# A two-layer trunk on one core: MLPs in groups of three pairs with products and up blocks in turn, and the attention's weights split in the first MLP

## The chip, the cores and the metric

The kernel runs on one core of a Trainium2 chip. The metric is the time of one execution on the device in microseconds, the median of the runs; lower is better. The kernel is written in Tile: a planner puts each engine's instructions in an order at build time and adds the semaphores, and on the chip every engine takes its instructions in that order.

Engines, as the profile names them: PE is TensorE (matmuls; PEld its weight loads), DVE is VectorE, ACT is ScalarE, POOL is GpSimd, SP is SyncE, which here issues all DMAs.

## The reference

The input is 512 tokens of 1024 channels, all float32. Layer 0 mixes tokens by pooling, layer 1 by stick-breaking attention with 16 heads of 64; each mixer is followed by an MLP with a hidden width of 4096. Every part has an RMS norm before and after it.

```python
def sq_relu_mlp(h, w_up, w_down):
    u = jnp.matmul(h, w_up)
    return jnp.matmul(jnp.square(jax.nn.relu(u)), w_down)
...
    for layer in range(DEPTH):
        h = rms_norm(x, mix_pre_g[layer])
        if layer < N_A:
            m = pool_mixer(h, pool_w[layer], pool_scale[layer])
        else:
            q = jnp.matmul(h, w_q[j]).reshape(B, S, N_HEADS, HEAD_DIM).transpose(0, 2, 1, 3)
            o = stick_breaking_attention(q, k, v)
            m = jnp.matmul(o.transpose(0, 2, 1, 3).reshape(B, S, HD), w_o[j])
        x = x + rms_norm(m, mix_post_g[layer])
        h = rms_norm(x, mlp_pre_g[layer])
        x = x + rms_norm(sq_relu_mlp(h, w_up[layer], w_down[layer]), mlp_post_g[layer])
        if layer == N_A - 1:
            kv = jnp.matmul(rms_norm(x, kv_norm_g), w_kv).reshape(B, S, 2, N_HEADS, HEAD_DIM)
...
```

## The kernel before

**Precision.** A float32 operand is split in two fp32r parts, high and low: ACT casts the high part (`split`, line 188, or `weight`, line 118), DVE subtracts it from the source for the low part (lines 189 and 120). Each product is three matmuls: high x high, high x low, low x high.

**Weights of up blocks and of the attention.** `weight` (line 106) loads 512 KB into one of two `raw` buffers (line 108, on SP), multiplies it by a gain on POOL where there is one (line 130, two instructions; the v, k and q weights of the attention have one, the o weights not), casts (118) and subtracts (120). The results go to one of four slots. `queue` holds all weights in the order of their use, first MLP, attention, second MLP; `fill` makes the next one as long as fewer than four are made and not yet used, `get` hands one out. In the attention, `fill` also keeps a weight's instructions behind the latest ones of the main work (`behind`, `gate`).

**An MLP** has 32 up blocks of 128 hidden units. An up block is 24 matmuls of 512 columns (lines 534 to 536), then Relu and Square on ACT (489, 490). The first 28 blocks' down product is done by a Strassen scheme (Winograd's form, seven products in place of eight) in the class `Seven`: seven groups of four blocks, that is of two pairs. The left operands are sums of the squares (tokens halved; lines 403 to 406 on POOL), the right ones combinations of quarters of four w_down blocks (line 423 on DVE), both then split by `split`. `feed` makes the left operands of a group as its up blocks come out, `prepare` the right ones. `add_to` (461) runs a group's seven products in a row: each is 12 matmuls (line 456) into two PSUM banks, followed by two instructions that add the banks to `y` (line 473, DVE; the first touch of a part is a copy on ACT, 471). Between two groups' products stand four up blocks. The last four blocks are multiplied plainly in `contract` (lines 209 to 211), which also runs the layer's end norm and update, tile by tile of 128 tokens. The w_down blocks of a group are loaded into the three `xn` buffers, which the norms use too, and a spare one (lines 382 to 384).

**The start of an MLP.** The first four up blocks are computed in two halves of the tokens, because the norm's last two token tiles are transposed late (`need`). Then comes a fifth up block, and then the first group's seven products.

**The attention** follows a list, `ATT_ORDER` (line 49): V (values), K and P (keys, queries), S (scores, sigmoids, the scan of line 752 on DVE), T (transposes, 770), A (mixing with the values, 780), O and E (output projection through `contract`, PE order kept by hand in E). Its 32 weights (8 each of v, k, q and o) are made one after the other by `fill` as slots come free.

Of the kernel before, what the change touches and what calls it, by code (L numbers as in the profile page):

```python
# [15 lines left out]
P = 128  # L16
D = 1024
# [5 lines left out]
GRP = 4  # L23
HEADS = 16
# [37 lines left out]
def trunk(ctx, tc, x, consts, gcol, grow, pw, wup, wdn, wq, wk, wv, wo, out):  # L62
# [5 lines left out]
    psum = pool("psum", 8, space=bass.MemoryType.PSUM)  # L68

# [19 lines left out]

    def xn_tile():  # L90
        return work.tile([P, D], F32, tag="xn", bufs=3, name=name("xn"))
# [49 lines left out]
    def place(k):  # L141

        if k[0] == "dn":
            return [dn_pool[0].tile([P, D], F32R, tag="w", bufs=8, name=name(x)) for x in "hl"]
        if k == ("o", 6):
            both = att_pool[0].tile([P, 2, D], F32R, tag="v", bufs=2, name=name("w"))
            return [both[:, 0], both[:, 1]]
        if k == ("o", 7):
            return [att_pool[0].tile([P, NSEG], F32R, tag="w", bufs=2, name=name(x))[:, :D] for x in "hl"]
        return [wts.tile([P, D], F32R, tag=f"w{x}", bufs=4, name=name(x)) for x in "hl"]  # L150

    def make():
        k, src, scaled = queue.pop(0)
        on = nc.gpsimd if k in ON_POOL else nc.vector
        made[k] = weight(src, place(k), scaled, on)

    def fill(n=1):
        if gate[0]:
            behind.update(latest)
        for _ in range(n):  # L160
            if queue and len(made) < ahead and (queue[0][0][0] != "dn" or dn_pool[0] is not None):
# [7 lines left out]
    for l in range(2):  # L169
        if l == 1:  # L170
            for what, i, part in ATT_ORDER:
# [6 lines left out]
                elif what == "O" and 0 in part or what == "E":  # L178
                    for c in range(2 * i, 2 * i + (2 if what == "O" else 4)):
                        want(("o", c), wo[c])  # L180
        for j in range(NJ):
# [111 lines left out]
    def contract(lhs, w, y, first, update=None, tiles=range(T), soon=False):  # L293
# [4 lines left out]
        for t in tiles:  # L298
# [26 lines left out]
            else:  # L325
                product(0, range(last + 1))
            evacuate(0)
# [5 lines left out]
            elif normed and t == T - 1:  # L333
                if not soon:
                    ups[0].transpose()
# [26 lines left out]
    class Seven:  # L362
# [11 lines left out]

        PRODUCTS = (
# [4 lines left out]
        def __init__(self, l, g, mp):  # L380
            self.mp, self.rows, self.left, self.right = mp, [], {}, {}
            self.raw = [xn_tile(), xn_tile(), xn_tile(), spare_tile()]
            for j, raw in enumerate(self.raw):
                nc.sync.dma_start(raw, wdn[l, g * GRP + j])
            self.rest = self.prepare()

        def feed(self, r):

            q, second = divmod(len(self.rows), 2)
            self.rows.append(r)  # L390
            tile = lambda n, tag: self.mp.tile([P, 2, n], F32R, tag=tag, bufs=2, name=name(tag))
            lo, hi = slice(0, S // 2), slice(S // 2, S)
            if not second:
                a = self.left["r11", q] = tile(S // 2, "r11")
                split(r[:, lo], a[:, 0], a[:, 1])
                return
            a = tile(S, "r2")
            split(r, a[:, 0], a[:, 1])
            self.left["r12", q], self.left["r22", q] = a[:, :, lo], a[:, :, hi]
            r1 = self.rows[-2]  # L400
            sums = self.mp.tile([P, 2, S], F32, tag="s", name=name("s"))
            s2, s3, s1, s4 = sums[:, 0, lo], sums[:, 0, hi], sums[:, 1, lo], sums[:, 1, hi]
            nc.gpsimd.tensor_tensor(out=s3, in0=r1[:, lo], in1=r1[:, hi], op=ALU.subtract)
            nc.gpsimd.tensor_tensor(out=s1, in0=r1[:, hi], in1=r[:, hi], op=ALU.add)  # L404
            nc.gpsimd.tensor_tensor(out=s2, in0=s1, in1=r1[:, lo], op=ALU.subtract)  # L405
            nc.gpsimd.tensor_tensor(out=s4, in0=r[:, lo], in1=s2, op=ALU.subtract)
            for n, (x, y) in enumerate((("s2", "s3"), ("s1", "s4"))):
                a = tile(S, f"s{n}")
                split(sums[:, n], a[:, 0], a[:, 1])
# [481 lines left out]
```

## Time and profile before

| What | Value |
|---|---|
| Median of 3 runs | 994.76 us (992.62 to 996.26) |
| The profiled execution's own time | 996.64 us |
| Its span, first to last instruction | 994.8 us |
| Mean granted TensorE clock | 0.984 |
| Stages, from the windows | pooling mixer to 56 us; first MLP to 372; attention to about 650; second MLP to the end |

A row of the windows table gives, for a stretch in us from the span's start, each engine's busy time and, in brackets, its number of instructions, then the clock granted to TensorE (1.00 is full), the mean busy share of the 16 DMA engines and GB/s moved. A row of a timeline gives start, duration, engine, line, operation, output<-inputs and, in square brackets, how long the engine sat idle before it and what ended that. A row of one line's durations gives min/median/max in ns.

### The profile page before, as it was taken

The numbers are of one execution on the slowest core, as the hardware profiler recorded it, in microseconds if no ns is written. First come the engines' busy times: TensorE is split into PE (matmuls) and PEld (weight loads), VectorE is DVE, ScalarE is ACT, GpSimd is POOL, SyncE is SP. The second block draws the span as 40 slices with busy tenths as digits, with TensorE's granted clock in tenths as the row PEclk, the third lists the DMA queues.
The fourth block names the chain that finished last, engine by engine and source line by source line (L and its number), as shares of the span: only waits on it lengthen the run. The fifth ranks groups of instructions, "written<-read, shape, count | busy, mean of one in ns | idle before, by whom it ended". The sixth has DMA issues, their size and how long they took to land.

```text
span 994.8 us, 12988 instructions
## 1 busy us (share of the span) xinstructions
PE 954.4 (96%) x4823; PEld 810.8 (82%) x4823; DVE 780.6 (78%) x1067; ACT 557.0 (56%) x1005; POOL 252.2 (25%) x238
## 2 busy tenths in 40 slices
PE   7898999999999999999999999989999999999997
PEld 5896888888888888888788988788888888888886
DVE  5987788878877747488688889989778878888636
ACT  5656546456455446566667576658556455464532
POOL 1642202112021147241252300436212021121103
PEclk8998999999999999999999999999999999999999
DMA  7254323323232230112222221144323233231202
GB/s 267 85 162 135 106 86 107 109 103 106 85 111 81 85 127 22 62 45 64 64 73 69 64 72 65 65 148 149 110 102 111 84 125 105 85 127 64 64 22 85
DMA packets 26991, 94.50 MB, mean 95 GB/s; under 512 B 3120, under 2 KB 3504, under 8 KB 26928
## 3 DMA queue, kind: packets, MB, share of 16 engines
q1 hardware_dynamic: 26928, 93.68, 28.2%
q8 instruction: 38, 0.62, 0.2%
q14 instruction: 25, 0.20, 0.1%
HBM read 91.57 MB, written 2.10 MB: 94 GB/s over the span
## 4 chain that ended last, share of the span: by engine, by line
PE 76%; DVE 8%; ACT 4%; POOL 3%; issue 2%; DMA 1%; POOLq 0%; DVEq 0%; ACTq 0%
PE ps L456 26%; PE ps L535 13%; PE ps L536 13%; PE ps L534 13%; PE ps L209 3%; PE ps L210 2%; PE ps L211 2%; DVE e L752 2%; PE ps L780 1%; DVE l L120 1%; PE ps L770 1%; POOL y L234 1%; DMA xn<-in_wdn 1%; ACT h L118 1%; DVE x L240 1%
## 5 line engine op out<-in xcount | busy, mean ns | idle before, releaser
L535 PE MATMUL ps<-xnl,h 128*128 128x512 f32 (+1 forms) x712 | 262.0, 369 | 4.1 <-DVE xnl L189 4.1
L536 PE MATMUL ps<-xnh,l 128*128 128x512 f32 (+1 forms) x712 | 262.1, 369 | 0.5 <-DVE l L120 0.5
L534 PE MATMUL ps<-xnh,h 128*128 128x512 f32 (+1 forms) x712 | 261.0, 369 | 0.0
L120 DVE TENSOR_TENSOR l<-raw,h 128x1024 fp32r<-128x1024 f32 x101 | 128.8, 1276 | 48.5 <-ACT h L118 48.3
L456 PE MATMUL ps<-w,s 128*128 128x512 f32 x672 | 163.4, 394 | 2.1 <-ACT s L188 1.5
L535 PEld LDWEIGHTS ps<-xnl,h 128*128 128x128 f32 x712 | 134.8, 189 | 26.1 <-DVE xnl L189 4.3
L536 PEld LDWEIGHTS ps<-xnh,l 128*128 128x128 f32 x712 | 134.8, 189 | 22.8 <-DVE l L120 0.7
L456 PEld LDWEIGHTS ps<-w,s 128*128 128x128 f32 x672 | 127.2, 190 | 31.1 <-ACT s L188 2.7
L534 PEld LDWEIGHTS ps<-xnh,h 128*128 128x128 f32 x712 | 134.2, 190 | 21.9
L473 DVE TENSOR_TENSOR y<-ps,y 128x512 f32<-128x512 f32 x180 | 120.1, 688 | 40.5 <-PE ps L456 39.3
L118 ACT CAST h<-raw 128x1024 fp32r<-128x1024 f32 x105 | 110.4, 1053 | 63.9 <-PE ps L535 32.4
L456 PE MATMUL ps<-w,r 128*128 128x512 f32 x504 | 124.3, 390 | 2.4 <-DVE r L189 2.4
L188 ACT CAST w<-t 128x512 fp32r<-128x512 f32 x112 | 69.2, 622 | 80.8 <-PE ps L456 61.0
L456 PEld LDWEIGHTS ps<-w,r 128*128 128x128 f32 x504 | 94.7, 188 | 22.4 <-DVE r L189 2.8
L404 POOL TENSOR_TENSOR s<-r,r 128x256 f32<-128x256 f32 x28 | 28.2, 1008 | 323.9 <-ACT r L490 323.9
L130 POOL TENSOR_TENSOR raw<-raw,gc 128x512 f32<-128x512 f32 x48 | 69.9, 1477 | 145.7 <-DMA raw<-in_wv 68.9
L188 ACT CAST w<-xn 128x512 fp32r<-128x512 f32 x56 | 34.9, 624 | 90.1 <-PE ps L456 80.0
L189 DVE TENSOR_TENSOR w<-t,w 128x512 fp32r<-128x512 f32 x112 | 76.5, 705 | 0.7 <-ACT w L188 0.7
L188 ACT CAST s<-s 128x512 fp32r<-128x512 f32 x56 | 34.6, 620 | 45.6 <-POOL s L405 37.6
L189 DVE TENSOR_TENSOR s<-s,s 128x512 fp32r<-128x512 f32 x56 | 42.5, 763 | 22.0 <-ACT s L188 17.5
L189 DVE TENSOR_TENSOR r<-r,r 128x512 fp32r<-128x512 f32 (+1 forms) x60 | 47.2, 789 | 11.7 <-ACT r L188 11.6
L752 DVE TENSOR_TENSOR_SCAN e<-u,begin 128x1280 f32<-128x1280 f32 x16 | 47.5, 2968 | 8.7 <-ACT u L746 8.5
(138 smaller groups left out, 1577.9 us busy)
## 6 DMA issues: line engine op xcount, KB each, us to landing
raw<-in_wup SPq DMA_DIRECT2D x64, 512.0 KB, 3.5
xn<-in_wdn SPq DMA_DIRECT2D x42, 512.0 KB, 3.6
spare<-in_wdn SPq DMA_DIRECT2D x14, 512.0 KB, 4.1
raw<-in_wdn SPq DMA_DIRECT2D x8, 512.0 KB, 3.5
raw<-in_wv SPq DMA_DIRECT2D x8, 512.0 KB, 3.4
raw<-in_wk SPq DMA_DIRECT2D x8, 512.0 KB, 3.5
raw<-in_wq SPq DMA_DIRECT2D x8, 512.0 KB, 3.5
raw<-in_wo SPq DMA_DIRECT2D x8, 512.0 KB, 3.5
```

What stands on the lines that cost most here:

```text
L118: nc.scalar.copy(hi, raw)
L120: on.tensor_tensor(out=lo, in0=raw, in1=hi.bitcast(F32), op=ALU.subtract)
L130: nc.gpsimd.tensor_tensor(out=v[:, h], in0=v[:, h], in1=g[:, h].broadcast_to((P, n // 2, D // n)), op=ALU.mult)
L188: latest["act"] = nc.scalar.copy(hi, src)
L189: latest["dve"] = nc.vector.tensor_tensor(out=lo, in0=src, in1=hi.bitcast(F32), op=ALU.subtract)
L209: nc.tensor.matmul(dst, ah, bh, start=start, stop=False)
L456: nc.tensor.matmul(bank, r[:, a], w_[:, NS[b]], start=start and q == 0 and k == 0, stop=q == 1 and k == 2, skip_group_check=True,)
L473: nc.vector.tensor_tensor(out=part, in0=bank, in1=part, op=ALU.add)
L534: nc.tensor.matmul(pu[:, cols], wh[:, k, :], xnh[:, k, cols], start=k == 0, stop=False)
L535: nc.tensor.matmul(pu[:, cols], wh[:, k, :], xnl[:, k, cols], start=False, stop=False)
L536: nc.tensor.matmul(pu[:, cols], wl[:, k, :], xnh[:, k, cols], start=False, stop=k == KC - 1)
L752: nc.vector.tensor_tensor_scan(out=e[:, ::-1], data0=u[:, 1:][:, ::-1], data1=begin[:, ::-1], initial=0.0, op0=ALU.mult, op1=ALU.max,)
```

## The change

**The MLP.** The 28 blocks of the Strassen part are cut into five groups, of 2, 3, 3, 3 and 3 pairs. The operands of one product for all pairs of a group are now made by single instructions: a left operand is one cast and one subtract over pairs x 256 columns, a right one a combination, a cast and a subtract over pairs x 512. They lie in two buffers each, so that the operands of product i+2 are made while product i+1 waits or runs; before, a group's operands were made in advance of all its products. A product of three pairs is 18 matmuls. After each product comes one up block of the next group, as long as there are any (six for seven products; in the last group the four plain blocks). The left sums are formed in place, four per group as before four per pair. The w_down blocks of a group come by two DMAs, one into an own tile `w1`, one into `xn3`, the three norm buffers in one tile.

**The attention's weights.** In the first MLP, after each product, `split_apart` loads, scales and splits one of the 32 attention weights into a single buffer `apart`; the next call writes it to DRAM (1 MB, both parts) before it takes its own weight. Groups 1 to 3 take a second one after their fourth product. In the attention, `make` only loads the two parts from DRAM (two DMAs of 512 KB) into a slot.

**What goes with it.** A weight's two parts lie in one tile; four plain w_down weights go into operand buffers that the last group has left; the attention keeps its mixed heads in buffers of its own; the DMA scratch is 256 in place of 1024; the first tile's transposes in the last norm are issued a little earlier.

```diff
+GROUPS = (2, 3, 3, 3, 3)
+MOST = max(GROUPS)
...
+    xn3 = work.tile([P, 3, D], F32, tag="xn3", name="xn3")
+    turn = [0]
+
     def xn_tile():
-        return work.tile([P, D], F32, tag="xn", bufs=3, name=name("xn"))
+        turn[0] += 1
+        return xn3[:, turn[0] % 3]
...
+    def split_apart(mp):
+        for both, t in going:
+            nc.sync.dma_start(both, t.bitcast(F32))
+        going.clear()
+        if not apart:
+            return
+        k, src, scaled = apart.pop(0)
+        t = mp.tile([P, 2, D], F32R, tag="apart", name=name("apart"))
+        weight(src, [t[:, 0], t[:, 1]], scaled)
+        kept[k] = dram.tile([P, 2, D], F32, tag=f"kept{len(kept)}", name=name("kept"))
+        going.append((kept[k], t))
 
     def make():
         k, src, scaled = queue.pop(0)
+        if k in kept:
+            made[k] = place(k)
+            for n, t in enumerate(made[k]):
+                nc.sync.dma_start(t.bitcast(F32), kept[k][:, n])
+            return
...
+        def load(self, second):
+            n = self.n
+            if second:
+                w = self.w2 = xn3
+            else:
+                w = self.w1 = self.mp.tile([P, MOST, D], F32, tag="w1", name=name("w1"))
+            src = wdn[self.l, self.first : self.first + 2 * n].rearrange("(n k) p d -> k p n d", k=2)
+            nc.sync.dma_start(w[:, :n], src[1 if second else 0])
...
+        def left(self, i):
+            n, key = self.n, self.PRODUCTS[i][1]
...
+            s1 = self.s1[:, :n]
+            sub = lambda out, x, y, op=ALU.subtract: nc.gpsimd.tensor_tensor(out=out, in0=x, in1=y, op=op)
+            if key == "s3":
+                sub(s1, r21, r22, ALU.add)
+                sub(r21, r11, r21)
+                sub(r11, s1, r11)
+            elif key == "r22":
+                sub(r11, r12, r11)
+            src = {"r11": r11, "s3": r21, "s2": r11, "r22": r22, "s1": s1, "r12": r12, "s4": r11}[key]
+            a = self.mp.tile([P, 2, MOST, S // 2], F32R, tag="a", bufs=2, name=name("a"))
+            split(src, a[:, 0, :n], a[:, 1, :n])
+            return a
+
+        def right(self, i):
...
+            if key == "t3":
+                combine(e, w22, w12)
+            elif key == "t2":
+                combine(e, e, w11, ALU.add)
+            elif key == "t4":
+                combine(e, w21, e)
+            elif key == "t1":
+                combine(w12, w12, w11)
...
+            w = self.mp.tile([P, 2, MOST, 512], F32R, tag="w", bufs=2, name=name("w"))
+            split(src, w[:, 0, :n], w[:, 1, :n])
+            return w
...
     def mlp(l, mp, update):
...
+        groups[0].load(0)
+        groups[0].squares()
         need(0, 1)
...
+        for i in range(2):
+            groups[0].make(i)
+        for g, group in enumerate(groups):
+            coming = groups[g + 1] if g + 1 < len(groups) else None
+            if coming:
+                coming.squares()
+            ups = list(range(firsts[g + 1], firsts[g + 1] + 2 * GROUPS[g + 1]) if coming else range(plain, NJ))
+            for i in range(7):
+                group.product(i, y, written if g == 0 else None)
+                if l == 0:
+                    for _ in range(2 if i == 3 and 0 < g < 4 else 1):
+                        split_apart(mp)
+                if i + 2 < 7:
+                    if ups:
+                        up(ups.pop(0))
+                    group.make(i + 2)
+                    if i + 2 == 4 and coming:
+                        coming.load(0)
+                    if i + 2 == 6 and coming:
+                        coming.load(1)
+                else:
+                    if ups:
+                        up(ups.pop(0))
+                    if coming:
+                        coming.make(i + 2 - 7)
...
```

More of the change, by code (lines that the diff above doesn't have):

```diff
@@ L378, in trunk @@
         )
[L380 to L391, printed above, removed]
-            lo, hi = slice(0, S // 2), slice(S // 2, S)
[L393 to L409, printed above, removed]
-                self.left[x, q], self.left[y, q] = a[:, :, lo], a[:, :, hi]
```

176 lines of the change are left out of this document (83 added, 93 removed).

## The prediction

> **What bounds the kernel now.** I read the page first, for the engines' shares. TensorE (PE) is the bound, 96% busy, VectorE (DVE) follows with 78%; the chain of waits says the same: 76% of it is PE, 8% DVE.
>
> ```profile
> PE 954.4 (96%) x4823; PEld 810.8 (82%) x4823; DVE 780.6 (78%) x1067; ACT 557.0 (56%) x1005; POOL 252.2 (25%) x238
> PE 76%; DVE 8%; ACT 4%; POOL 3%; issue 2%; DMA 1%; POOLq 0%; DVEq 0%; ACTq 0%
> ```
>
> An average hides the stages, so next the table by windows (busy us and count of each engine, granted clock, DMA share, GB/s).
>
> ```profile
> core 0: us, PE busy (x) PEld busy (x) DVE busy (x) ACT busy (x) POOL busy (x), PEclk, DMA share, GB/s
> 56.00:84.00 28.00, 25.04 (x165) 22.24 (x163) 25.34 (x30) 17.45 (x30) 11.90 (x9) 0.97 0.45 145
> 84.00:124.80 40.80, 40.76 (x168) 32.86 (x168) 29.22 (x43) 25.14 (x44) 7.53 (x8) 0.93 0.32 111
> 124.80:165.60 40.80, 40.80 (x181) 33.78 (x180) 33.43 (x48) 21.41 (x36) 6.96 (x8) 1.00 0.31 104
> 410.00:510.00 100.00, 95.64 (x533) 82.54 (x532) 78.62 (x75) 65.90 (x132) 32.58 (x21) 1.00 0.22 69
> 510.00:530.00 20.00, 16.75 (x104) 15.10 (x103) 16.16 (x20) 12.38 (x25) 10.46 (x8) 0.91 0.24 79
> 530.00:630.00 100.00, 98.39 (x575) 86.40 (x574) 89.05 (x96) 64.98 (x130) 11.19 (x9) 1.00 0.20 67
> 630.00:650.00 20.00, 17.29 (x83) 13.51 (x81) 19.45 (x32) 14.02 (x33) 14.13 (x12) 1.00 0.18 66
> 650.00:690.00 40.00, 36.40 (x250) 34.31 (x251) 35.13 (x51) 24.96 (x45) 19.57 (x13) 0.96 0.49 158
> 690.00:930.00 240.00, 240.00 (x1060) 198.47 (x1059) 193.23 (x279) 129.37 (x210) 47.32 (x49) 1.00 0.30 101
> ```
>
> Two things are to be seen. In steady MLP (124.8 to 165.6, 690 to 930) PE has no gap: a group of two pairs takes 40.8 us for 84 product and 96 up matmuls, 0.227 us each. The change has the same 14 pairs and 28 + 4 blocks, so the same matmuls: **there is nothing to win in steady MLP, only to lose.** All that can be won lies in the other windows: at the first MLP's start, in the attention, and at its end.
>
> **The change, part by part.**
>
> (1) *The first MLP's start.* PE waits here for DVE:
>
> ```profile
> 83.00 1.22 PE L456 MATMUL ps<-w,r 128*128 128x512 f32 x2 [2.42 <-DVE r L189]
> 78.47 1.20 PE L456 MATMUL ps<-w,s 128*128 128x512 f32 x4 [0.54 <-DVE s L189]
> 84.26 1.35 PEld L456 LDWEIGHTS ps<-w,s 128*128 128x128 f32 x4 [0.76 <-ACT s L188]
> ```
>
> That is 3.7 us, and a stretch at half clock follows: the window from 84 holds 168 matmuls where the next one holds 181, and 13 x 0.227 = 3.0 us. Together 6.7. DVE is late because the operands of seven products and five up blocks' weights are wanted in one lump (25.3 of 28 us busy). The new order needs two products' operands first and the rest two products later. But product 0 now follows the fourth up block at once, without a fifth between (24 x 0.227 = 5.4 us of cover gone): it needs the last square's split, and product 1 a chain of three POOL sums. Bounds: −6.7, and +2 if that chain shows. I take **−4**.
>
> (2) *Steady MLP, the engines behind PE.* Durations (min/median/max) and, for pipelining, two in a row:
>
> ```profile
> L189 DVE TENSOR_TENSOR w<-t,w x112: 679/686/1224, 63.4 to 937.1; 128x512 fp32r<-128x512 f32 x112
> L120 DVE TENSOR_TENSOR l<-raw,h x101: 1193/1225/2304, 16.1 to 952.4; 128x1024 fp32r<-128x1024 f32 x101
> L756 DVE TENSOR_TENSOR w<-w,e x16: 1472/1490/2081, 424.7 to 609.0; 128x1280 f32<-128x1280 f32 x16
> 85.14 1.28 DVE L189 TENSOR_TENSOR s<-s,s 128x512 fp32r<-128x512 f32 x2
> L473 DVE TENSOR_TENSOR y<-ps,y x180: 679/687/693, 95.3 to 951.8; 128x512 f32<-128x512 f32 x180
> L118 ACT CAST h<-raw x105: 1034/1050/1216, 15.0 to 951.1; 128x1024 fp32r<-128x1024 f32 x105
> L130 POOL TENSOR_TENSOR raw<-raw,gc x48: 1035/1042/3553, 350.9 to 567.7; 128x512 f32<-128x512 f32 x48
> L404 POOL TENSOR_TENSOR s<-r,r x28: 733/774/4480, 71.1 to 927.1; 128x256 f32<-128x256 f32 x28
> ```
>
> A 512-wide DVE instruction takes 0.69 but the next starts 0.60 after it; so I count 0.60 for 512 and 1.14 for 1024, and from the slope between 512 and 1280 (0.80 us in 768) 0.33 for 256, 0.87 for 768 and 1.67 for 1536. The trace has no 1536: it lies between the 1280 row's 1.49 and three of 512 (1.80); 1.67 is on the line through the rows. Before, a group's 48 DVE instructions are 14 evacuations, 14 right splits and 8 combinations of 512 (21.6), 8 left splits (4.3) and 4 up weights (4.6): 30.5 of 40.8 us; the window shows 33.4, a tenth more by waiting. After, a group of three pairs (61.2 us): 14 evacuations 8.4, 7 right splits 11.7, 4 combinations 6.7, 7 left splits 6.1, 6 up weights 6.8 = 39.7, that is 65% where it was 75%. Evacuations fall from 98 to 70 in an MLP. So in the second MLP DVE has more room than before; PE's cover for an operand is product + up, 18 + 24 matmuls, 9.5 us, against some 4 us of cast and subtract. I cost it at **0**; bound +5, if the double buffers (one product ahead where it was a group) let a wait through.
>
> (3) *The 32 weights moved into the first MLP.* Each brings a 512 KB load, for 24 of them two POOL multiplies (2.1 us), a cast (1.05), a subtract (1.14) and a 1 MB write, and fetches 1 MB back in the attention. By the attention's order 7 fall in group 0 (all with gains), 8 (6 with), 8 (all), 8 (3) in groups 1 to 3, one in group 4. With eight, DVE has 39.7 + 9.1 = 48.8 of 61.2 us: 80%, as much as before (82% in the window). ACT is far from full. The narrow places are two.
>
> The two raw buffers. With ACT and DVE nearly free, three weights with gains followed each other like this:
>
> ```profile
> 354.10 1.23 DVE L120 TENSOR_TENSOR l<-raw,h 128x1024 fp32r<-128x1024 f32 x1 [3.10 <-ACT h L118]
> 358.79 1.22 DVE L120 TENSOR_TENSOR l<-raw,h 128x1024 fp32r<-128x1024 f32 x1 [2.02 <-ACT h L118]
> 363.48 1.23 DVE L120 TENSOR_TENSOR l<-raw,h 128x1024 fp32r<-128x1024 f32 x1 [2.02 <-ACT h L118]
> raw<-in_wup SPq DMA_DIRECT2D x64, 512.0 KB, 3.5
> out<-x SPq DMA_DIRECT2D x7, 256.0 KB, 2.0
> ```
>
> 4.69 us each; a weight without gains holds a buffer for 3.5 + 1.05 + 1.2 + 0.3, so one every 3.0. Eight with gains and six up weights: 37.5 + 18 = 55.5 of 61.2 us. It fits, with little left for queueing; the four up weights made ahead are a cushion of four steps (38 us). The DMA engines: 36 pieces of 0.52 MB in 61.2 us is 308 GB/s, and by the window's 0.31 at 104 GB/s a share of 0.9. A 1 MB write has no row: above 2.0 (256 KB) and below 7.0 (two loads of 512 KB); I take 5. It is waited for: one *apart* tile, so the next cast waits for its landing, and behind that cast stand Relu, Square and the operands' casts on ACT; SP's write waits for the subtract, and the raw loads stand behind it. At one weight a step (9.5 us), cast, subtract and write (7.3) fit.
>
> The second is that DVE and POOL hold each other up:
>
> ```profile
> 414.27 3.02 POOL L130 TENSOR_TENSOR raw<-raw,gc 128x512 f32<-128x512 f32 x2 [16.76 <-DMA raw<-in_wv]
> 414.44 1.95 DVE L120 TENSOR_TENSOR l<-raw,h 128x1024 fp32r<-128x1024 f32 x1 [1.37 <-ACT h L118]
> ```
>
> Multiplies of 1.04 and a subtract of 1.22 became 3.02 for two and 1.95. POOL's work in a group with eight gained weights: four sums of 768 (between 1.04, the 512 row, and 3 x 0.77; I take 1.34) 5.4, and 16 x 1.04 = 16.7: 22 us, beside 40.4 us of DVE with both inputs in SBUF. 62.4 of 61.2 if they exclude each other wholly. How much of it is queued shows only the window from 124.8, where 7 us of POOL cost DVE under 3. I take **+2** for the first MLP, bounds 0 and +27 (rival B).
>
> On this the Trainium skill, SBUF — State Buffer, section "Who interferes with whom", says that a DVE instruction with two SBUF inputs and a GpSimd one that reads SBUF exclude each other for the whole instruction. The two rows agree with it; it would turn +2 into rival B's sum.
>
> (4) *The attention.* It loses 32 casts, 31 subtracts and 48 multiplies. PE's waits there, 400 to 640 (total us, times, longest):
>
> ```profile
> PE ps L209 <- DVE kl L694: 1.9, 2, 1.4
> PE ps L780 <- ACT ah L188: 1.7, 1, 1.7
> PE ps L780 <- DVE al L189: 1.6, 2, 0.9
> PE ps L738 <- DVE q L703: 1.0, 1, 1.0
> PE ps L780 <- DVE v L655: 0.8, 1, 0.8
> ```
>
> All are short DVE or ACT instructions late in a queue in which the weight splits stand (the five and five smaller: 9.3). The windows from 410 to 630 give 9.2 us of idle PE, and the 0.91 of 510 to 530 another 1.8: 11 us. Without 1.14 x 31 = 35 us of splits in some 240, DVE falls from 84% to 69%. Against it: a fetched weight can start only when its slot's matmuls are over (two 512 KB loads, about 5 us) where a split took 2.3 out of a buffer already filled. Bounds −11 and +3; I take **−7**.
>
> (5) *Hand-over to the second MLP.* Idle PE 2.7 + 3.6 in 630 to 690, the largest this wait, while DVE sat in a 2.30 us subtract of an up weight against a POOL multiply:
>
> ```profile
> PE ps L535 <- DVE xnl L189: 4.1, 1, 4.1
> 647.43 2.30 DVE L120 TENSOR_TENSOR l<-raw,h 128x1024 fp32r<-128x1024 f32 x1
> ```
>
> Up weights are still split there. Bounds −6 and +2; I take **−3**.
>
> (6) *Tails.* After the last group's fourth product no up block stands between products 4, 5 and 6: the operand of product 6 (cast, subtract, about 4.3 us with the left one) has product 5's 4.1 us. **+1** for both MLPs; bounds 0 and +4.
>
> The sum: −4 + 0 + 2 − 7 − 3 + 1 = **−11**. The profiled execution took 996.6 us (span 994.8 and 1.8 around it): 985.6 for its like. It lies 1.9 over the median of 994.8, so against the median: **984**.
>
> **The rivals.**
> *A, the forecast*: 984, between 977 and 989.
> *B, slower: the first MLP is bound by DVE and POOL together.* If POOL overlaps neither the evacuations nor idle DVE, groups 0, 1, 2 take 57.2, 66.7 and 70.8 us for PE's 51.7, 61.2 and 61.2: 5.5 + 5.5 + 9.6 = +20.6 in place of +2, and 984 + 18.6 = 1002; with two half-clock stretches as at 84 (3.0 each) 1008. A late raw buffer or *apart* write would show at the same place. For it: POOL's 22 of 61 us with DVE at 80%. Against: DVE spends 8.4 us of each group reading PSUM, and idles a tenth. It decides from 13 us lost on, two thirds of the price.
> *C, no difference: the attention's waits are the length of chains (cast, subtract, scan), not load.* Then −7 becomes 0 and −3 becomes −1: 993. For it: DVE has 36 of these 220 us free already.
> *D, all waits go*: −6.7 − 11 − 6 = −24: 971.
>
> **How the numbers follow.** A 0.50, B 0.27, C 0.13, D 0.10. A measurement of this kernel tells about 0.5% (5 us) from no change. Of A 0.05, of B 0.05 and of C 0.10 end within it; C's other 0.03 and B's 0.22 are slower. Faster 0.55, same 0.20, slower 0.25. For 8 in 10 the range reaches from D to B: 971 to 1006.
>
> **What would show it.** Right: matmul counts per group window in both MLPs at 0.227 us each; no wait of PE over 1 us around the first product; no POOL multiply in the attention, DVE there near 70%, and PE's waits of list (4) mostly gone. Wrong: PE waits on left or right operands (or up weights) in groups 0 to 2 with POOL busy and DVE subtracts of 2 us; granted clock under 0.95 in first-MLP windows; PE waiting for fetched weights in the attention; DVE over 90% anywhere in steady MLP.

## The result and the profile after

The changed kernel takes **1045.75 us** (1044.99 to 1049.6, 4 runs) against 994.76: a ratio of 1.052 (95% interval 1.049 to 1.055). It is slower by 51 us; the forecast was 984. The profiled execution has a span of 1043.7 us.

The page after, engines' shares, chain of waits, granted clock in 40 slices and the writes of the moved weights:

```profile
PE 963.3 (92%) x4823; PEld 814.3 (78%) x4823; DVE 731.5 (70%) x771; ACT 526.2 (50%) x837; POOL 231.5 (22%) x166
PEclk8999999898998899889999999999999999999998
PE 57%; DMA 14%; DVE 11%; ACT 5%; POOL 4%; issue 3%; SPq 0%; POOLq 0%; ACTq 0%; DVEq 0%
kept<-apart SPq DMA_DIRECT2D x32, 1024.0 KB, 4.8
```

No engine is fuller than before: DVE fell from 78% to 70%, POOL from 25% to 22%. PE's own part of the chain fell from 76% to 57%, and transfers have 14% where they had 1%. So the loss is in waits, not in work; but for the last slice, the slices with a low clock are all among the first 18 of 40.

The stages, cut at their first and last matmul, in us of one profiled execution each. The first MLP is here counted to the last matmul of its plain blocks, 387 us in the kernel before, later than the 372 in the table of stages above. The executions of one kernel differ by 3 us or so, and such lengths with them.

| | mixer | first MLP | attention | second MLP | end |
|---|---|---|---|---|---|
| before | 44.6 | 342.6 | 260.3 | 340.3 | 7.0 |
| after | 44.7 | 412.5 | 242.0 | 335.2 | 9.3 |
| difference | +0.1 | **+69.9** | **−18.3** | −5.1 | +2.3 |

Windows of after: first MLP, attention, the steady part of the second MLP, then two pieces of the first (us, PE, PEld, DVE, ACT, POOL busy and count, granted clock, DMA share, GB/s):

```profile
44.70:457.20 412.50, 355.00 (x1576) 289.32 (x1575) 287.03 (x266) 201.12 (x261) 134.23 (x84) 0.93 0.61 214
457.20:699.20 242.00, 241.56 (x1441) 214.75 (x1440) 168.82 (x207) 137.23 (x305) 17.24 (x31) 1.00 0.37 129
726.00:1008.00 282.00, 282.00 (x1248) 233.37 (x1247) 201.72 (x176) 137.30 (x165) 47.32 (x20) 1.00 0.30 100
72.56:124.00 51.44, 51.44 (x227) 42.58 (x228) 36.56 (x33) 30.40 (x41) 18.98 (x14) 1.00 0.71 255
312.00:372.00 60.00, 45.58 (x179) 35.63 (x177) 30.52 (x25) 21.69 (x25) 18.79 (x13) 0.86 0.66 228
```

The new order by itself keeps PE full: 282.00 of 282 us in the second MLP. In the first MLP PE idles 57.5 us (4.8 before), and the rest of the loss is clock: its 1576 matmuls are busy for 355 us, where they were busy for 337.8. In the attention PE idles 0.4 us. The first group of the first MLP (72 to 124) is still full; the stretch from 312 runs 179 matmuls where 264 fit (60 / 0.227), with DVE half idle and the DMA share at 0.66. Over this stretch neither is full; something between them is waited for.

PE's waits in the first MLP of after (total us, times, longest):

```profile
PE ps L582 <- ACT w L127: 22.6, 5, 9.6
PE ps L313 <- ACT xn L304: 9.9, 1, 9.9
PE ps L241 <- ACT dn L127: 5.7, 2, 5.2
PE ps L486 <- DVE w L221: 5.7, 3, 4.6
PE ps L584 <- DVE w L129: 4.1, 3, 3.7
```

The largest is an up weight's cast (L127) and subtract (L129): 26.7 us. Two more, 15.6 us, stand at the MLP's end (w_down weights of the plain blocks, norm), and the rest are the products' operands, as in the row of L221. What an up weight waits for is seen in the longest of them, in the timelines of SP, POOL, ACT and PE (start, duration, what; in brackets the idle time before):

```profile
315.82 0.33 SPq L117 DMA_DIRECT2D raw<-in_wup  x1
328.19 0.33 SPq L117 DMA_DIRECT2D raw<-in_wv  x1
329.32 0.33 SPq L167 DMA_DIRECT2D kept<-apart  x1
329.75 0.37 SPq L117 DMA_DIRECT2D raw<-in_wv  x1
337.60 0.33 SPq L167 DMA_DIRECT2D kept<-apart  x1
338.03 0.37 SPq L117 DMA_DIRECT2D raw<-in_wup  x1
```

```profile
332.07 2.04 POOL L139 TENSOR_TENSOR raw<-raw,gc 128x512 f32<-128x512 f32 x2 [5.30 <-DMA raw<-in_wv]
...
335.27 1.04 ACT L127 CAST apart<-raw 128x1024 fp32r<-128x1024 f32 x1 [7.42 <-DMA kept<-apart]
...
342.49 1.04 ACT L127 CAST apart<-raw 128x1024 fp32r<-128x1024 f32 x1 [5.02 <-DMA kept<-apart]
343.66 1.04 ACT L127 CAST w<-raw 128x1024 fp32r<-128x1024 f32 x1
```

```profile
344.76 0.80 PE L582 MATMUL ps<-xnh,w 128*128 128x512 f32 x1 [9.55 <-ACT w L127]
```

Two moved v weights hold both raw buffers from 328.19 and 329.75. ACT idles 7.42 us before the first one's cast. Its load and its two multiplies take up most of that, to 334.11; the landing of the write before it, which the profile names, adds the last 1.2 us. Only after the subtract, at 338.03, can the next up weight's load be issued, 22 us after the one before, where a step of the MLP takes 9.5. It lands at 343.64 and is cast at once, at 343.66. PE waits 9.55 us and then runs at half clock. The up weight before it was late for another reason: its load, issued at 315.82, landed at 325.84, 10.0 us later, while the DMA share from 316 to 324 was 0.96.

Over the whole window 72 to 412 the loads and subtracts in the trace pair up to 58 weights through the two buffers, each held 11.7 us on average: 678 of 2 x 340 us. The ring is full all the time. That alone shows nothing: paired in the same way, the two buffers of the kernel before are held for 99.9% of 84 to 340, and there PE has next to no wait, since a load goes out as soon as a buffer is free and the weight then lies there. What differs is how long it lies. Before, of the 23 up weights loaded from 82 to 315, none was cast sooner than 3.5 us after its landing, and the mean was 14.8 us. In after, 18 of the 25 loaded from 72 to 412 were cast within 0.5 us of it. **The ring of two raw buffers has no slack left.**

### The profile page after: what moved, and what is told of

It is laid out like the page before. It is cut to its first block, busy times and chain, and to the rows that moved or that the text cites. A ratio compares the mean times of both kernels' runs of the same rounds, so it can differ in the third digit from the quotient of the medians.

```text
span 1043.7 us, 12411 instructions
## 1 busy us (share of the span) xinstructions
PE 963.3 (92%) x4823; PEld 814.3 (78%) x4823; DVE 731.5 (70%) x771; ACT 526.2 (50%) x837; POOL 231.5 (22%) x166
## 4 chain that ended last, share of the span: by engine, by line
PE 57%; DMA 14%; DVE 11%; ACT 5%; POOL 4%; issue 3%; SPq 0%; POOLq 0%; ACTq 0%; DVEq 0%
PE ps L486 15%; PE ps L584 9%; PE ps L582 9%; PE ps L583 9%; DMA raw<-in_wup 6%; DMA kept<-apart 4%; PE ps L241 3%; PE ps L242 3%; PE ps L243 3%; DVE apart L129 2%; PE ps L828 2%; DVE w L129 2%; PE ps L818 2%; DMA raw<-in_wo 2%; POOL raw L139 2%
## 5 line engine op out<-in xcount | busy, mean ns | idle before, releaser
L486 PE MATMUL ps<-w,a 128*128 128x512 f32 x1176 | 286.4, 396 | 14.2 <-DVE w L221 5.7
L582 PE MATMUL ps<-xnh,w 128*128 128x512 f32 (+1 forms) x712 | 263.8, 373 | 22.6 <-ACT w L127 22.6
L486 PEld LDWEIGHTS ps<-w,a 128*128 128x128 f32 x1176 | 224.2, 192 | 65.7 <-DVE w L221 7.1
L584 PE MATMUL ps<-xnh,w 128*128 128x512 f32 (+1 forms) x712 | 263.9, 371 | 4.1 <-DVE w L129 4.1
L583 PE MATMUL ps<-xnl,w 128*128 128x512 f32 (+1 forms) x712 | 263.9, 371 | 1.1 <-DVE xnl L221 1.1
L582 PEld LDWEIGHTS ps<-xnh,w 128*128 128x128 f32 x712 | 135.0, 191 | 46.7 <-ACT w L127 24.7
L584 PEld LDWEIGHTS ps<-xnh,w 128*128 128x128 f32 x712 | 135.2, 190 | 29.2 <-DVE w L129 6.6
L583 PEld LDWEIGHTS ps<-xnl,w 128*128 128x128 f32 x712 | 135.8, 191 | 23.4 <-DVE xnl L221 1.3
L129 DVE TENSOR_TENSOR w<-raw,w 128x1024 fp32r<-128x1024 f32 x62 | 80.7, 1304 | 53.9 <-ACT w L127 53.8
L266 POOL TENSOR_TENSOR y<-y,grow 128x512 f32<-128x512 f32 x12 | 17.8, 1493 | 335.2 <-ACT xn L224 335.2
L127 ACT CAST w<-raw 128x1024 fp32r<-128x1024 f32 x66 | 68.8, 1044 | 27.2 <-DMA raw<-in_wup 26.0
L129 DVE TENSOR_TENSOR apart<-raw,apart 128x1024 fp32r<-128x1024 f32 x32 | 43.5, 1361 | 46.2 <-ACT apart L127 46.1
L221 DVE TENSOR_TENSOR a<-r,a 128x768 fp32r<-128x768 f32 (+1 forms) x60 | 65.5, 1092 | 9.8 <-ACT a L220 9.6
L441 POOL TENSOR_TENSOR s<-r 128x768 f32<-128x768 f32 (+1 forms) x10 | 22.1, 2208 | 220.2 <-ACT r L517 220.2
L127 ACT CAST apart<-raw 128x1024 fp32r<-128x1024 f32 x32 | 33.6, 1049 | 70.9 <-DMA kept<-apart 38.2
L221 DVE TENSOR_TENSOR w<-e,w 128x1536 fp32r<-128x1536 f32 (+1 forms) x30 | 60.5, 2016 | 7.8 <-ACT w L220 7.6
```

The source lines that it names most:

```text
L127: nc.scalar.copy(hi, raw)
L129: on.tensor_tensor(out=lo, in0=raw, in1=hi.bitcast(F32), op=ALU.subtract)
L221: latest["dve"] = nc.vector.tensor_tensor(out=lo, in0=src, in1=hi.bitcast(F32), op=ALU.subtract)
L486: nc.tensor.matmul(bank, a[:, x, q, TS[t]], w[:, z, q], start=start and q == 0 and k == 0, stop=q == self.n - 1 and k == 2, skip_group_che ...
L582: nc.tensor.matmul(pu[:, cols], wh[:, k, :], xnh[:, k, cols], start=k == 0, stop=False)
L583: nc.tensor.matmul(pu[:, cols], wh[:, k, :], xnl[:, k, cols], start=False, stop=False)
```

## The experiments

The theories, numbered as in the expectations where they have numbers: theory 1, the ring of two raw buffers that moved weights share with up weights; theory 2, the waited-for 1 MB writes; theory 3, DMA engines that are too full; theory 4, the POOL multiplies against DVE; against all of them, that the regrouped MLP itself costs the time. Ratios are to the kernel before on the same chip; where none is given there was one run.

**No weight moved.**

```diff
-            apart.extend(queue[n:])
```

> No weight is split in the first MLP; the attention splits its own, as before; the MLP is that of the changed kernel. If the moved weights are the loss (all four theories below share this), the first MLP runs at PE's pace again, and the time is 985 to 995 us: the first MLP 338 to 342 us long instead of 412, the attention again about 266. If instead the new MLP order itself stalls PE (operands one product ahead), the first MLP stays above 360 us and the time above 1010.

999.66 us, ratio 1.0056 (1.0037 to 1.0075); first MLP 348.4, attention 257.3. So 64.1 of the 69.9 us (412.5 − 348.4) come with the moved weights, as all theories had it, but the time misses the 985 to 995 that was expected. The other 5.8 are a loss of 11.5 at the first MLP's end less 5.7 won at its start: after 1500 of its matmuls e1 stands at 320.0 us and before at 325.7, and the rest takes 28.4 us in place of 16.9. Waits of this kernel there:

```profile
PE ps L312 <- ACT xn L303: 11.2, 1, 11.2
```

The transposes for the attention wait 11.2 us for the norm, and the first 2.9 us after that run at half clock.

**A raw buffer of their own for the moved weights** (a tile that lies idle in the MLP).

```diff
-        weight(src, [t[:, 0], t[:, 1]], scaled)
+        weight(src, [t[:, 0], t[:, 1]], scaled, raw=spare_tile())
```

> The moved weights are loaded into a buffer of their own (the spare row buffer), the up weights keep both raw buffers. Theory 1 (the ring of two raw buffers: 64 weights that hold one for 11 us each are 350 us for a stage of 300): PE's waits for up weights (27 us in the changed kernel, with the half-clock stretches behind them) go, the time falls by 30 us or more, to 970 to 1015. Theory 2 (the next cast waits on ACT for the write of the single split buffer) and theory 3 (the DMA engines are too full): the same bytes, writes and waits remain, so under 15 us are won, 1030 or more. Theory 4 (DVE and POOL hold each other up): nothing is won, 1040 or more.

1004.23 us, ratio 1.0096 (1.0073 to 1.0119): 41.5 us less than after, first MLP 361.2. PE's waits and ACT's longest in this kernel:

```profile
ACT apart L128 <- POOL spare L140: 97.9, 23, 6.8
...
PE ps L487 <- DVE a L222: 6.8, 3, 2.3
...
ACT w L128 <- DMA raw<-in_wup: 0.9, 1, 0.9
```

No wait of PE for an up weight is left, and after the first, no up weight is cast sooner than 2.5 us after its landing. Theory 1 holds: the first MLP is 51.3 us shorter with the same weights, bytes, writes and multiplies. The own buffer is itself full (32 holds are 367 of the 381 us from 54 to 435), but now only moved weights stand in its line. They fall behind: three are loaded after the first MLP's end, and the attention is 247.7 us long. A moved weight's cast waits 97.9 us in all on ACT, with the operands' casts behind it; that the waits for operands that PE has left come from there is argued, not shown.

**Only the first weight written** (it is then read for all 32; the ring stays shared), and **no gain multiplies for the moved weights** (their gains are left out).

```diff
+        if kept:
+            kept[k] = next(iter(kept.values()))
+            return
```

> Only the first moved weight is written to DRAM; the other 31 writes are left out, and the attention reads that one weight 32 times, so its values are not the reference's. All loads, multiplies, casts and subtracts stay. Theory 2: the 38 us in which ACT waited for writes go, and with them most of the loss: under 1005. Theory 3: half of the moved bytes go, DMA share falls from 0.65 to under 0.5 and the time to under 1010. Theory 1: only the loads get faster (about 1.5 of 11 us of a hold), 1020 to 1040. Theory 4: 1040 or more.

```diff
-        weight(src, [t[:, 0], t[:, 1]], scaled)
+        weight(src, [t[:, 0], t[:, 1]])
```

> The multiplies by the gains are left out for the moved weights (48 POOL instructions; values differ slightly from the reference's). Theory 4: the loss goes, under 1000. Theory 1: holds of 24 of 64 weights get 3 to 4 us shorter, so the ring needs some 45 us less, and the time is 1000 to 1015. Theories 2 and 3: writes and bytes stay, 1035 or more.

1015.89 and 1014.68 us: 30 and 31 less than after. The first falls between what theories 1 (1020 to 1040) and 2 (under 1005) gave, and above theory 3's 1010; the second fits theory 1 and neither theory 4 nor theories 2 and 3. The savings in the first MLP, with that of e2, are 51.3, 33.4 and 30.8 us, together far more than the 64.1 that there are: they are links of one chain. A write, a multiply and a shared buffer each lengthen the hold of a raw buffer, and with no slack in the ring a shorter hold shortens every step. Neither run alone gives the ring its slack back: the up weights still lie 0.8 and 0.7 us on average between landing and cast.

**The first 16 weights only**, one after every second product, ring shared.

```diff
-            apart.extend(queue[n:])
+            apart.extend(queue[n : n + 16])
```

> The shared ring of two raw buffers as in the changed kernel, but only the first 16 of the 32 weights are moved, one after every second product. Theory 1: 48 in place of 64 weights at 11.7 us each need 280 us of two buffers, less than the stage has, so the first MLP falls from 412 to 350 to 355 us; the attention gets back half of its gain (250 to 256): 1000 to 1005. If each moved weight costs the same by itself (16 x 1.4 us of a loss of 45), it is 1020 to 1025.

1008.1 us, first MLP 363.8: 16 weights cost 15 us over e1, 32 cost 64. It lies above the 1000 to 1005 that theory 1 gave. The cost per weight doubles as the ring fills; it isn't zero below that. Here an up weight lies 4.0 us on average before its cast, and 7 of 24 are cast within 0.5 us.

**The w_down weights of the plain blocks asked for earlier**, without moved weights: first two of the four after the last group's fourth product; then also the third, into the tile that the moved weights would use, with the second half of the w_down blocks loaded in two pieces a step earlier and two products exchanged so that its first half is free in time.

```diff
+                    if i == 3 and not coming:
+                        w, e = piece("w1", 3), piece("e", 1)
+                        dn_pool[0] = [[w[:, 0], w[:, 1]], [w[:, 2], e[:, 0]]]
+                        fill(2)
```

> No weight is moved (as in the run of the MLP alone, 999.7 us), and the four plain w_down weights of an MLP's end are asked for two products earlier, the first two already after the last group's fourth product. Theory of the tail (these weights come too late, the planner then orders the plain product bank by bank in parallel, all its evacuations and norms come in one lump, and PE waits 11.3 us for the first transposes, with 10 us at half clock behind it): the wait shrinks below 3 us and the time is 985 to 991. Rival (the lump comes from the transposes that the change issues earlier in the last norm): nothing changes, 998 to 1001.

996.67 us, ratio 1.0015 (0.9999 to 1.0032): 3 us where 9 to 15 were expected, with a wait of 9.1 us left. The weights came hardly earlier: the first two were cast at 333.7 and 334.6 (334.0 and 334.9 in e1), and the last two still waited for a buffer of the seventh product and were cast at 352.7 and 353.7. The last subtract ended at 362.4, and the first finished bank of the plain product was taken up by DVE at 367.2, after that weight had come.

> No weight is moved; the MLP with the early second half and the plain w_down weights in buffers that are free earlier. Theory of the tail (the last plain weight, which waited for the seventh product's buffer, orders the end): the wait for the first transposes falls from 9 to under 3 us and the time is 986 to 991. Rival (the tail has another cause): 995 to 998.

988.13 us, ratio **0.9917** (0.9899 to 0.9935), first MLP 338.5. The waits at its end, for the same place as the 11.2 us above:

```profile
PE ps L312 <- ACT xn L303: 2.3, 2, 1.7
```

So 9.9 us of the first MLP (348.4 − 338.5) were its end (after 1500 matmuls it takes 17.6 us more, not 28.4), and the regrouped MLP with that mended is 0.8% faster than the kernel before. Which of the run's parts did it was not taken apart.

**Two own buffers** (`own_tile` gives the idle tile and the gain row's, which is then loaded later), then **with e5's earlier weights**, and the **two own buffers with the earlier second half of the w_down blocks**.

> The moved weights get two raw buffers of their own in turn (the two spare row buffers; the row of gains that one of them held is loaded at the MLP's end). Theory 1 (buffers): with one own buffer each weight held it 12.1 us for a step of 9.5, so the moved weights themselves were still late; with two the first MLP falls from 361 to 350 us and the time from 1004 to 985 to 995. Rival (DMA engines, or DVE and POOL holding each other up, are what is left): under 5 us are won, 999 to 1006.

> Two own raw buffers and the earlier w_down weights together. If both theories hold and their terms add: first MLP 338 to 345, attention 242 to 247, MLP 2 335 to 339, the time 968 to 982, faster than before. If only the tail's holds: about 992. If neither: 1000 to 1005.

> The run with two own raw buffers (1006.6 us), and the second half of the w_down rows of a group is loaded in two pieces, the one that product 1 needs a step earlier (products 5 and 6 change places, so that its buffer half is free a step earlier). Theory: what is left there is mostly this load, late once per group (PE waits of 4.1, 5.2 and 3.7 us at the groups' second products and half clock behind each): they go, first MLP 371 to 357 us, the time 990 to 995. Rival (the in-order queues behind the moved weights stall PE wherever it has least cover): the waits move elsewhere, 1000 or more.

1006.58 (1.0108, 1.0086 to 1.013), 1005.41 (1.0102, 1.0076 to 1.0128) and 1002.3 (1.0068, 1.0044 to 1.0092). None reached what its theory gave. The first two ended within 0.6 us of the range that stood for nothing won, and e11 in that of its rival, by which the waits move elsewhere. Of e6:

```profile
ACT apart L134 <- DMA kept<-apart: 74.6, 22, 5.7
...
PE ps L493 <- DVE w L228: 12.4, 3, 5.0
DVE e L467 <- DMA xn<-in_wdn: 11.0, 5, 3.1
```

The second buffer moved the cast's wait from POOL to the write and bought nothing: the attention is 5.6 us shorter than in e2, since no moved weight falls behind, and the first MLP 9.4 longer. PE's three waits of 12.4 us stand within the first product of the last three groups, and not at the second as was expected. DVE, in order, has the second product's combination ahead of the first one's subtract, and that combination waits for the second half of the w_down blocks, late from DRAM. Asked for earlier (e11), those waits went and one for DVE's additions into `y` came (7.5 us): 4 us.

**All of it together**: e11, e10's end, one weight after each product (28), each write in two halves.

> Two own raw buffers, the early second half, 28 of the 32 weights moved (the last four o weights are split in the attention), one after each product, each written in two halves, and the four plain w_down weights in buffers that are free earlier. If buffers and loads are all of the loss: first MLP 340 to 346, attention 243 to 247, 972 to 980. If a moved weight still costs by the queues it stands in: 990 to 1000.

997.81 us, ratio 1.0027 (1.001 to 1.0044): the second of the two ranges expected. First MLP 362.4, attention 243.7. Against e10 the 28 weights cost 23.9 us (0.85 each) in the first MLP and save 17.9 in the attention, even with their own buffers. By the medians the net cost is 9.7 us and not 6: the profiled execution of e10 took 2.9 us more than its median and that of e9 2.0 less, so a saving or a cost read against e10's stages is uncertain by some 3 us. Two runs ask what the 23.9 are: e9 with only the first weight written, and e9 without the gains.

> The run with 28 moved weights in own buffers (997.8 us; its first MLP 362 us, 24 more than without moved weights), but only the first weight is written to DRAM and read again for all 28, so values are not the reference's. Theory 2 in its small form (ACT waits 61 us, in order, for writes out of the single split buffer, and casts and Relus of the main work stand behind): the 24 us fall under 8, the time under 983. Theory 4 (DVE and POOL): the 24 us stay above 16, 990 or more.

> The same with all writes, but without the gains' multiplies on POOL for the moved weights (values differ from the reference's). Theory 4: the 24 us fall under 8, the time under 983. Theory 2: they stay above 16, 990 or more. Both parts: each run between, 983 to 990.

1001.13 (1.0063, 1.0036 to 1.009), no faster, as theory 4 had it: the writes cost nothing any more. 987.04 (0.9914, 0.9884 to 0.9945), first MLP 349.4: without the multiplies 13.0 of the 23.9 go; 10.9 are left where theory 4 gave under 8, and the time is in the range that stood for both parts. The stretch 84 to 344 of the first MLP in e10, e9, e12 and e13:

```profile
84.00:344.00 260.00, 260.00 (x1149) 215.36 (x1148) 188.86 (x164) 125.85 (x149) 40.55 (x16) 1.00 0.31 102
```

```profile
84.00:344.00 260.00, 244.45 (x1046) 198.64 (x1045) 221.29 (x173) 135.87 (x161) 120.21 (x57) 0.98 0.73 253
```

```profile
84.00:344.00 260.00, 242.11 (x1036) 197.04 (x1036) 216.12 (x170) 135.50 (x160) 109.99 (x57) 0.97 0.46 148
```

```profile
84.00:344.00 260.00, 254.12 (x1101) 207.93 (x1100) 208.44 (x182) 143.05 (x170) 41.09 (x17) 0.99 0.75 261
```

Without moved weights (first row) PE is full. Taking out the writes (third) lowers the DMA share from 0.73 to 0.46 and PE gains nothing; taking out the multiplies (fourth) leaves the share at 0.75, and PE has 9.7 us more. So the multiplies cost time here, and the writes don't. The traces put it on DVE: in e9 a multiply takes 2.0 us in the median, where 1.04 is its least, DVE is busier with fewer instructions, and PE waits for its additions into `y`, which e13 hardly does (e9 first):

```profile
PE ps L498 <- DVE y L507: 7.7, 2, 4.1
PE ps L498 <- DVE y L507: 0.4, 2, 0.2
```

ACT's long waits for the writes are not it: they stay in e13, 66.1 us where e9 has 60.9. The other 10.9 us (349.4 − 338.5) were not split further; in e13 PE's waits are for operands of products, 2.1 us at the longest.

**Fewer weights**: e9 with the first 12; and e9 with 16, the eight o weights, which have no gain, and eight with gains.

```diff
-            apart.extend(queue[n : n + 28])
+            apart.extend([q for q in queue[n:] if q[2] is None] + [q for q in queue[n:] if q[2] is not None][:8])
```

> Twelve moved weights, one after the products 0, 2 and 4 of a group, in own buffers. If what a moved weight costs is queueing that a sparser stream escapes, the first MLP stays within 3 us of the 338.5 without moved weights and the attention wins 5 to 8 us: 980 to 985, the fastest of all. If each costs 0.85 us at any rate (24 of 28), the time is 988 to 993.

> Sixteen moved weights, four a group, in own buffers: the eight o weights, which have no gains and so no work on POOL, and the first eight with gains. If what is left of a moved weight's cost is mostly the POOL multiplies against DVE (13 of 24 us), the first MLP stays within 5 us of 338.5 and the attention wins 8 to 10: 983 to 987. If the cost is by weight whatever it holds, 988 to 992.

987.97 us (0.9921, 0.9902 to 0.994), where 980 to 985 was expected of a sparser stream: by the stages, 12 weights cost 2.5 us and save 6.4, but the time is that of e10, 988.13. **985.58 us (0.9898, 0.9879 to 0.9916)**, the lowest time of all and below both kernels: 16 weights cost 10.4 us, double what was expected, and save 13.1. Its interval overlaps that of e10, so it isn't shown that moving any weight pays. Nor do the multiplies alone set the price: e14's 12 weights all have gains and cost less than these 16, of which 8 have none. Here one wait of 5.7 us for DVE's additions into `y`, with half clock around it, is most of the cost; why DVE is late there was not looked into.

## Why the prediction was wrong

(1) *First MLP's start*, −4: right. The first product of after waits 1.8 us, so its chain does show a little, and the clock in 72 to 124 is 1.00 with 227 matmuls, where before lost 6.7: about −5.

(2) *Steady MLP*, 0: right. PE 282.00 of 282, DVE 201.72 of it, 72% where 65% was worked out: again a tenth more, as in the window of before that the prediction read. The sizes were right. The 1536-wide subtract was taken at 1.67 and the 768-wide at 0.87, counted to the start of the next instruction, and with 0.09 added for the overlap these are the medians, 1.76 and 0.95. The tenth is in few instructions: from 726 to 1008 fourteen took up to twice their median, all of them beside one of POOL's, 16 us in all. Rows of after:

```profile
L221 DVE TENSOR_TENSOR w<-e,w x30: 1215/1756/3466, 68.8 to 979.8; 128x1536 fp32r<-128x1536 f32 x24, 128x1024 fp32r<-128x1024 f32 x6
L221 DVE TENSOR_TENSOR a<-r,a x60: 680/951/2005, 72.5 to 1005.2; 128x768 fp32r<-128x768 f32 x48, 128x512 fp32r<-128x512 f32 x12
L441 POOL TENSOR_TENSOR r<-r x20: 1287/2032/3468, 76.1 to 972.0; 128x768 f32<-128x768 f32 x16, 128x512 f32<-128x512 f32 x4
```

(3) *The moved weights*, +2: **this step failed.** It measured +64 (e1 against after), beyond its upper bound of 27. The failing sentence is on the raw buffers: "55.5 of 61.2 us. It fits, with little left for queueing." The 55.5 came from durations of a stretch in which ACT and DVE were nearly free. An up weight's load, taken at 3.5 us, took 5.6 in the median in this stretch at a DMA share of 0.64, and 6.2 on average:

```profile
raw<-in_wup SPq DMA_DIRECT2D x25, 512.0 KB, 5.6
```

and the waits that the same step named (ACT's cast behind the write, SP's loads behind the write's issue) were left out of the hold. In after they were:

```profile
SPq L167 <- DVE apart L129: 175.2, 31, 14.1
```

```profile
ACT apart L127 <- DMA kept<-apart: 38.2, 11, 7.4
...
ACT w L127 <- DMA raw<-in_wup: 24.2, 8, 7.4
ACT apart L127 <- POOL raw L139: 19.4, 7, 6.9
```

By the 55.5, a weight with gains holds a buffer for 9.4 us and an up weight for 6.05. In after a moved weight held it for 13.1 us (5.7 of load, 4.3 from landing to cast, 3.0 for cast and subtract) and an up weight for 10.0, nearly all of it load, cast and subtract. At such holds eight and six weights need 82 us of two buffers (half of 8 x 13.1 + 6 x 10.0), and a group at PE's pace has 61.2: a ring worked out at 91% full was over its limit. Part of these holds is itself waiting that the full ring causes, so 82 is too much as a size; that the shared buffer is the failed term is shown by e2, which takes 51.3 of the 64.1 us back. The cushion of four up weights doesn't help against a rate: the stretches 72 to 124 and 124 to 186 still ran full or nearly so, and then late loads reached PE. The write's own length (4.8, taken at 5) was right. The DMA share came to 0.64 over the stage, where 0.9 was worked out for a group of eight at PE's pace; DMA was full only at times, as from 316 to 324, and with own buffers taking the writes out bought nothing (e12).

Rival B had the right stage and named "a late raw buffer" as a thing that would show at the same place, but its priced mechanism, DVE and POOL excluding each other, is the smaller part. What it is worth with own buffers is seen in e13: 13 us with 28 weights, against 20.6. Here the Trainium skill, SBUF — State Buffer, section "Who interferes with whom", agrees in kind: 40 fewer POOL multiplies and 12.9 us less of DVE's busy time in the same stretch, though DVE ran 9 more instructions. The rule taken for all of POOL's time gave too much; that part of the multiplies fell beside DVE's other work is the likely reason, and no run shows it.

(4) *Attention*, −7: right in mechanism, too small, and (5) *hand-over*, −3: right. DVE fell to 70% (168.82 of 242), as worked out, and of PE's waits there are left:

```profile
PE ps L583 <- DVE xnl L221: 1.1, 1, 1.1
PE ps L313 <- ACT xn L304: 1.0, 2, 0.8
PE ps L241 <- ACT xnh L220: 0.2, 1, 0.2
```

The two stages together gave −23.4 (−18.3 and −5.1) against −10. Against e1, which has the new MLP and splits the attention's weights where before does, the attention saves 15.3. The attention's windows of before, whole and its first stretch:

```profile
387.20:647.50 260.30, 248.56 (x1441) 217.63 (x1440) 211.23 (x237) 165.96 (x335) 73.69 (x70) 0.99 0.20 64
387.20:410.00 22.80, 20.97 (x156) 20.35 (x155) 10.44 (x19) 11.18 (x24) 7.83 (x23) 0.93 0.07 24
```

The bound of −11 counted idle PE and one slow stretch; idle fell by 11.3 (260.30 − 248.56 = 11.7 to 0.4), but PE's busy time fell by 7.0 more for the same 1441 matmuls. The granted clock, 0.93 here and 0.91 from 510 to 530, and 1.00 throughout after, gives about 3.4 of these (22.8 x 0.07 + 20 x 0.09); the rest is open. Rival C is refuted, since the waits went with the load. A fetched weight, the feared wait, was never late.

(6) *Tails*, +1: wrong in size. e1 against before shows 11.5 us at the first MLP's end, beyond the bound of 4, and e10 wins 9.9 of them back; the step looked only at products 4 to 6 and not at the plain blocks' weights, which now wait for operand buffers of those products. The stretch after the second MLP's last matmul is 2.3 us longer.

Of the four signs that the prediction named for being wrong, two came: waits on up weights and operands in the first MLP's groups, with DVE subtracts of over 2 us beside POOL, and a clock under 0.95 there.

## What to carry to other kernels

Before work is moved under a bound engine, count the holds of every small buffer ring that it shares, from issue of the load to the last reader, with the load's time at the DMA share that the change will bring and with each wait in between; here a ring at 91% by unloaded durations was over its limit. Whether a ring is the limit is not told by how full it is, but by how long a landed buffer lies before its first reader. A wait inside an engine's queue (a cast behind a write) is passed on to everything behind it; whether it reaches the bound engine depends on what stands there (in e13 ACT has 66 us of such waits, and PE 9 us of waits from all causes). So moved work gets its own buffers, and only as much is moved as the covering stage has idle slots for: here 12 weights cost 2.5 us, within what the stage lengths differ by, 28 cost 0.85 each, 32 through the shared ring 2.0 each. A change of several parts is best run part by part: here one part alone is worth −0.8% once its end is mended, and the other cost 46 us (1045.75 − 999.66).

## What the runs showed of the hardware that was not expected

A short wait can cost more than its length. In after, a wait of 2.04 us is followed by a slow stretch. PE's timeline:

```profile
205.83 1.20 PE L486 MATMUL ps<-w,a 128*128 128x512 f32 x4
209.08 7.31 PE L486 MATMUL ps<-w,a 128*128 128x512 f32 x24 [2.04 <-DVE a L221]
```

The 24 matmuls took 7.31 us where 24 x 0.227 = 5.4: 1.9 us more, and the window 206 to 213 has a granted clock of 0.76 after 1.00 in the one before. The Trainium skill, TensorE: Matmul & The Clock Gate, section "What's actually happening", puts half clock after at least one idle window of about 3.4 us; in this run 2.04 us were enough. The length alone doesn't decide: in before, the 1.83 us of idle PE up to 399.4 are followed by half clock from 400.04 to 403.45, while in e2 waits of 2.26 and 2.31 us (windows 268 to 276 and 334 to 342) left the clock at 1.00. The half-clock stretches in after's first MLP are 3.4, 6.8 or 10.2 us long, steps of 3.4, so it seems to matter where a wait falls against these steps; that was not tested. The same 1576 matmuls of the first MLP were busy for 355.0 us where they took 337.8 before: 17 us of the 69.9 are put down to the clock after waits, 53 are the waits.

The POOL sums of 768 columns, 1.34 us by the prediction's estimate, took 1.84 us at the least and 2.5 in the median from 726 to 1008; the least of 1.287 in the row of L441 above is of a 512-wide one. So the estimate was short even for an undisturbed sum. How much of the rest is DVE's doing is not shown, since no run changed the width by itself.
